# Layer 0's first projection in three parts with a border for each group of columns, x's squares first and on two engines, and five modulation chunks fetched without waiting for a buffer

## The chip, the cores and the metric

One core of a Trainium2 chip runs the whole program; the core has five engines with a queue of instructions each. TensorE (PE in the profile) multiplies matrices into PSUM, VectorE (DVE), ScalarE (ACT) and GpSimd (POOL) work element by element, and SyncE (SP) issues all DMAs here. The metric is the time of one execution on the device in microseconds (us).

## The reference

Two layers on x (256 tokens by 2048 channels, float32). What matters here is the first step of layer 0: a modulation vector from c, then the normalised and modulated h, then one wide projection of h.

```python
mod = c_act @ ada_w[l] + ada_b[l]                       # 6 x 2048 values
sh_a, sc_a, gt_a, sh_m, sc_m, gt_m = jnp.split(mod, 6)
h = rmsnorm(x, norm_mix[l]) * (1.0 + sc_a) + sh_a
qa, ka, va, qb, kb, vb, ga, gb = split_cols(h @ w_in[l])
...                                                     # two attentions, projections
merged = jax.nn.sigmoid(ga) * ya + jax.nn.sigmoid(gb) * yb
x = x + gt_a * (merged @ w_out[l])
h = rmsnorm(x, norm_ffn[l]) * (1.0 + sc_m) + sh_m
...                                                     # gated MLP with a convolution of width 3
```

## The kernel before

Channels lie on the 128 partitions: x and h are 16 chunks (kc 0 to 15) of 128 channels by 256 tokens. Products in float32 quality are made of three products: each operand is split into a high part and a rest, and high x high, high x rest and rest x high are added up.

**Weights** come as a stream of units: one unit is 16 blocks of 128x128, 1 MB, one DMA (L255). ACT copies each half of a unit to its high part (`hl`, L264) and DVE subtracts that from the weights for the rest (`hl`, L265). There are 4 such halves in buffers, so two units at most are split ahead of PE. A unit costs PE 24 matmuls of 512 columns (`tokens`, L331 to L333, for q, k and v: tokens on the partitions of the result) or 48 of 256 columns (`features`, L273 to L275, for the gates and the rest).

**Modulation** is not on PE: for each of 96 chunks of 128 values DVE multiplies a 1 MB chunk of `ada_w` (`aw`, 128x2048) by silu(c) and adds along the row (L196). Chunks come in the order shift 0, scale 0, shift 1, scale 1 and so on, so that h of chunk kc needs `aw` number 2kc and 2kc+1. The rows of `aw` and the units of weights share one pool of four 1 MB buffers (`raw`): a DMA into it is issued when DVE has read the buffer's last content.

**The start.** ACT squares x in four pieces (L611), DVE adds them up and folds them (L613, L615), PE sums over the partitions (L618), DVE adds epsilon (L619), POOL takes the power -0.5 (L394), PE spreads it over the partitions (L385) and ACT copies it out (`rbs`, L389). Then each chunk of h is one step of `normed`: DVE makes `ht` (L403), ACT adds the shift and rounds to the high part of h (L406), DVE makes the rest (L407).

**Layer 0's first projection.** The columns are nine groups of 512 (k and v of the first attention, then q, and so on) and 16 blocks of gate A. Since h comes chunk by chunk, the sum over kc is cut into four parts, of 2, 4, 5 and 5 chunks. In each part all nine groups and all 16 gate blocks get the products of these chunks. The first part's results are copied to SBUF by ACT (L751, L787), the later ones are added there by DVE (L753, L782). The last part then goes on to the norms of q and k, their transposes, the attention heads (in the background) and the sigmoid of the gates. So part 0 is 4.5 + 2 = 6.5 units, and all parts together are 52. Ahead of each part the code brings h up to the part's last chunk; in between, a background job makes 0.65 of a chunk of `aw` per unit. A scheduler puts each engine's instructions into a fixed order when the program is built; at run time each engine goes through its list and waits wherever an operand isn't there.

## Time and profile before

| | us |
|---|---|
| median of 3 runs (lowest, highest) | 2703.92 (2703.27, 2705.94) |
| the profiled execution | 2704.2 |
| its span | 2702.4 |
| PE busy in the span | 2660.9 (98%) |
| DVE busy | 2099.4 (78%) |
| ACT busy | 1411.0 (52%) |

PE is busy nearly throughout, so what can be lost or won lies where it isn't, or where its matmuls start further apart than elsewhere. In the view by stretches each row has a stretch in us, then for each engine its busy us and, in brackets, its instructions; then the clock that TensorE was granted, the share of the DMA engines' time and GB/s. In the view in order of time a row has start, length, engine, line, operation, result<-operands and, in square brackets, how long the engine had sat idle before and what ended that. The chain of waits names start, length and what stood on the path.

### The profile page before, as it was taken

To read this page: it belongs to the slowest core of one execution; us is meant where nothing else is said; L and a number is where in the kernel's file an instruction comes from. 1 tells how busy PE (TensorE), PEld (TensorE's weight loads), DVE (VectorE), ACT (ScalarE), POOL (GpSimd) and SP (SyncE) were. 2 spreads that over 40 slices of the span, in tenths; PEclk is the share of its full clock that TensorE was granted. 3 is DMA by queue.
4 is the path that set the end of the run, shared out by engine and by line. 5 is a ranking of instruction groups with operands and counts; after the bars stand their busy time and mean duration, and the time that the engine had idled before them with its cause. 6 is when DMAs were issued, how large, how long until landed. Compare 5 with 4: busy or idle time off the path is not lost.

```text
span 2702.4 us, 50217 instructions
## 1 busy us (share of the span) xinstructions
PE 2660.9 (98%) x21088; PEld 2565.8 (95%) x21088; DVE 2099.4 (78%) x2941; ACT 1411.0 (52%) x2081; POOL 35.1 (1%) x24
## 2 busy tenths in 40 slices
PE   7899999999999999999999999999999999999999
PEld 5688799999999999999998889999999999999999
DVE  6998987897987888788886666658879866655664
ACT  5344684455754455345564556544565445543553
POOL 0000100000000000000000000000000000000000
PEclk9899999999999999999999999999999999999999
DMA  8887578987688888878766656666757775555554
GB/s 319 329 340 272 218 288 313 356 309 265 235 296 297 291 293 286 296 290 297 291 217 250 241 209 231 233 237 254 292 184 283 285 265 197 188 200 190 190 200 142
DMA packets 101892, 700.38 MB, mean 259 GB/s; under 512 B 12705, under 2 KB 15009, under 8 KB 17697
## 3 DMA queue, kind: packets, MB, share of 16 engines
q1 hardware_dynamic: 101666, 697.17, 70.7%
q8 instruction: 165, 2.70, 0.4%
q14 instruction: 61, 0.50, 0.0%
HBM read 695.03 MB, written 2.10 MB: 258 GB/s over the span
## 4 chain that ended last, share of the span: by engine, by line
PE 91%; DVE 4%; DMA 1%; ACT 1%; POOL 1%; issue 1%; SPq 0%; POOLq 0%; ACTq 0%; DVEq 0%
PE ps L273 26%; PE ps L275 25%; PE ps L274 25%; PE ps_t L332 4%; PE ps_t L333 4%; PE ps_t L331 4%; DVE aw L196 1%; DVE hl L265 1%; PE po L559 1%; PE sc L528 1%; DMA aw<-in_aw 1%; POOL qrs L378 1%; PE tp L553 0%; ACT hl L264 0%; DVE qn L492 0%
## 5 line engine op out<-in xcount | busy, mean ns | idle before, releaser
L265 DVE TENSOR_TENSOR hl<-w,hl 128x1024 fp32r<-128x1024 f32 x928 | 1130.2, 1222 | 362.5 <-ACT hl L264 360.9
L264 ACT CAST hl<-w 128x1024 fp32r<-128x1024 f32 x928 | 971.1, 1049 | 771.9 <-PE ps L275 487.1
L273 PE MATMUL ps<-h,hl 128*128 128x256 f32 x3328 | 925.1, 278 | 0.0
L275 PE MATMUL ps<-h,hl 128*128 128x256 f32 x3328 | 923.6, 278 | 0.9 <-DVE hl L265 0.9
L274 PE MATMUL ps<-h,hl 128*128 128x256 f32 x3328 | 921.9, 277 | 0.0
L275 PEld LDWEIGHTS ps<-h,hl 128*128 128x128 f32 x3328 | 625.4, 188 | 1.5 <-DVE hl L265 1.3
L273 PEld LDWEIGHTS ps<-h,hl 128*128 128x128 f32 x3328 | 625.9, 188 | 0.5
L274 PEld LDWEIGHTS ps<-h,hl 128*128 128x128 f32 x3328 | 625.3, 188 | 0.4
L196 DVE CUSTOM_DVE_ANT_0 aw<-aw,cact,ab 128x2048 f32<-128x2048 f32 x192 | 450.8, 2348 | 62.8 <-DMA aw<-in_aw 62.0
L331 PE MATMUL ps_t<-hl,h 128*128 128x512 f32 x576 | 227.4, 399 | 7.9 <-ACT hl L264 7.3
L332 PE MATMUL ps_t<-hl,h 128*128 128x512 f32 x576 | 228.4, 397 | 5.2 <-DVE hl L265 5.2
L333 PE MATMUL ps_t<-hl,h 128*128 128x512 f32 x576 | 228.1, 396 | 0.9 <-DVE h L407 0.9
L858 DVE SCALAR_TENSOR_TENSOR u<-ps,cw,u 128x255 f32<-128x255 f32 x304 | 146.2, 481 | 68.0 <-ACT u L856 64.0
L856 ACT ACTIVATE u<-ps,cw 128x256 f32<-128x256 f32 x152 | 85.7, 564 | 185.6 <-PE ps L275 185.4
L275 PE MATMUL ps<-merged,hl 128*128 128x256 f32 x512 | 142.1, 278 | 0.0
L274 PE MATMUL ps<-merged,hl 128*128 128x256 f32 x512 | 141.8, 277 | 0.0
L273 PE MATMUL ps<-merged,hl 128*128 128x256 f32 x512 | 141.8, 278 | 0.0
L274 PE MATMUL ps<-act_o,hl 128*128 128x256 f32 x512 | 141.6, 277 | 0.0
L275 PE MATMUL ps<-act_o,hl 128*128 128x256 f32 x512 | 141.6, 276 | 0.0
L273 PE MATMUL ps<-act_o,hl 128*128 128x256 f32 x512 | 141.4, 277 | 0.0
L331 PEld LDWEIGHTS ps_t<-hl,h 128*128 128x128 f32 x576 | 109.5, 190 | 31.9 <-ACT hl L264 8.4
L332 PEld LDWEIGHTS ps_t<-hl,h 128*128 128x128 f32 x576 | 109.8, 191 | 30.9 <-DVE hl L265 8.2
(209 smaller groups left out, 4574.1 us busy)
## 6 DMA issues: line engine op xcount, KB each, us to landing
w<-in_ws SPq DMA_DIRECT2D x464, 1024.0 KB, 4.9
aw<-in_aw SPq DMA_DIRECT2D x192, 1024.0 KB, 5.7
bias<-in_bias SPq DMA_DIRECT2D x16, 256.0 KB, 4.5
x<-in_xT SPq DMA_DIRECT2D x4, 512.0 KB, 5.4
out<-x SPq DMA_DIRECT2D x16, 128.0 KB, 2.3
cw<-in_cw SPq DMA_DIRECT2D x2, 176.0 KB, 4.5
maskA<-in_maskA SPq DMA_DIRECT2D x1, 256.0 KB, 5.3
ab<-in_ab SPq DMA_DIRECT2D x2, 48.0 KB, 6.1
```

The source lines that it names most:

```text
L196: nc.vector.tensor_tensor_reduce(out=raw[:], in0=raw[:], in1=cact[:], scale=1.0, scalar=ab[:, i : i + 1], op0=ALU.mult, op1=ALU.add, accum ...
L264: nc.scalar.copy(hl[:, 0], r)
L265: nc.vector.tensor_tensor(out=hl[:, 1], in0=r, in1=hl[:, 0].bitcast(F32), op=ALU.subtract)
L273: nc.tensor.matmul(out, hi, act[0], start=first, stop=False)
L274: nc.tensor.matmul(ps[:, :S], hi, act[1], start=False, stop=False)
L275: nc.tensor.matmul(out, lo, act[0], start=False, stop=last)
L331: nc.tensor.matmul(ps[:], xh, hi, start=kc == kcs[0], stop=False)
L332: nc.tensor.matmul(ps[:], xh, lo, start=False, stop=False)
L333: nc.tensor.matmul(ps[:], xl, hi, start=False, stop=kc == kcs[-1])
L378: nc.gpsimd.tensor_tensor(out=dst, in0=src, in1=mhalf[:, :k], op=ALU.pow)
L856: nc.scalar.activation(out=u, in_=ps, func=AF.Identity, scale=w[:, 1:2], bias=w[:, 3:4])
L858: nc.vector.scalar_tensor_tensor(out=u[:, to], in0=ps[:, of], scalar=w[:, j : j + 1], in1=u[:, to], op0=ALU.mult, op1=ALU.add)
```

## The change

- **Parts and borders.** Layer 0 has three parts, and each group of columns has its own border between them: the first part takes kc 0 to 1 for the first three groups, 0 to 2 for two, 0 to 3 for four and 0 to 5 for the gates; the second goes on to 8, 8, 9, 10, 10, 11, 10, 10, 12 and 13. The first part is now 28/4 + 6 = 13 units, the second 15 + 7 = 22, the third 14 + 3 = 17, 52 as before. Every group waits for the chunks of h that it needs itself (`have_h`).
- **Rates.** The background job makes 1.1, 0.85 and 0.7 chunks per unit in the three parts.
- **Start.** x's squares carry high priority; pieces 0 and 2 are squared by ACT, 1 and 3 by DVE; epsilon is added by ACT; 8 and 12 idle matmuls (`warm`) stand before and after the sum over the partitions.
- **Buffers.** `aw` chunks 2, 3 and 4 of layer 0 are read into room that the outputs (`o`, `b1`) need only later, and the first unit of weights is fetched after `aw` 1.
- The small tables (mask, rotation, gains) are loaded in the second part.

```diff
-K_PARTS_0 = [2, 4, 5, 5]
-K_PARTS = [[range(sum(K_PARTS_0[:i]), sum(K_PARTS_0[: i + 1])) for i in range(len(K_PARTS_0))], [range(KC)]]
+K_ENDS = [
+    [([2, 2, 2, 3, 3, 4, 4, 4, 4], 6), ([8, 8, 9, 10, 10, 11, 10, 10, 12], 13), ([KC] * 9, KC)],
+    [([KC] * 9, KC)],
+]
+def k_parts(l):
+    parts, at, gat = [], [0] * len(QKV_GROUPS), 0
+    for ends, gend in K_ENDS[l]:
+        parts.append(([range(a, e) for a, e in zip(at, ends)], range(gat, gend)))
+        at, gat = ends, gend
+    return parts
...
-FIRST_RATE = 0.65
+FIRST_RATE = [1.1, 0.85, 0.7]
...
-WARM_IN = 6
+WARM_IN = [8, 12, 6]
+OWN = {2: "o", 3: "o", 4: "b1"}
...
         for n, i in enumerate(ADA_ORDER):
-            raw = rawp.tile([P, D], F32, name=f"aw{l}_{n}", tag="raw")
+            if l == 0 and n in OWN:
+                if OWN[n] not in own:
+                    own[OWN[n]] = [place(OWN[n], 16 if OWN[n] == "o" else 12, F32, f"aw_{OWN[n]}"), 0]
+                t, k = own[OWN[n]]
+                own[OWN[n]][1] += 1
+                raw = t[:, KC // 2 * k : KC // 2 * (k + 1)].rearrange("p k s -> p (k s)")
+            else:
+                raw = rawp.tile([P, D], F32, name=f"aw{l}_{n}", tag="raw")
...
-        nc.scalar.activation(out=sq[:], in_=x[:, i : i + 4], func=AF.Square)
+            if i // 4 % 2:
+                nc.vector.tensor_tensor(out=sq[:], in0=x[:, i : i + 4], in1=x[:, i : i + 4], op=ALU.mult)
+            else:
+                nc.scalar.activation(out=sq[:], in_=x[:, i : i + 4], func=AF.Square)
...
-    nc.vector.tensor_scalar(out=mean_sq[:], in0=ps[:], scalar1=EPS, scalar2=None, op0=ALU.add)
+        nc.scalar.activation(out=mean_sq[:], in_=ps[:], func=AF.Identity, bias=eps[:])
...
-            while done[0] < 2 * len(K_PARTS[0][0]):
+            while done[0] < 2:
+                next(job0)
+            st.prefetch(1)
+            while done[0] < 2 * K_ENDS[0][0][0][0]:
                 next(job0)
...
+        def have_h(part):
+            while l == 0 and done[0] < 2 * part.stop:
+                next(job0)
+        for pi, (groups, gates) in enumerate(parts):
             last = pi == len(parts) - 1
-            for g in range(len(QKV_GROUPS)):
+            if l == 0:
+                bg.pace(job0, FIRST_RATE[pi])
+            for g, part in enumerate(groups):
+                have_h(part)
                 pss = st.tokens(h, part)
-                if pi == 0 and g == 0:
+                if pi == max(0, len(parts) - 2) and g == 0:
                     gains, sink, cw, rots = small(l)
```

In the order lists below a name has its numbers: `aw0_5` is chunk 5 of layer 0, `w0_2` unit 2 of its weights, `hl0_2_1` the second half of unit 2, `ps0_7_t0` a result for the first 128 tokens; the last number only tells buffers apart.

SP's queue, from the first chunk of `aw` on. Before:

```order
L195 DMA aw0_0_150<-in_aw 128x2048
L195 DMA aw0_1_153<-in_aw 128x2048
L195 DMA aw0_2_175<-in_aw 128x2048
L195 DMA aw0_3_178<-in_aw 128x2048
L255 DMA w0_0_192<-in_ws 128x2048
L145 DMA maskA_212<-in_maskA 128x512
```

Now:

```order
L219 DMA aw0_0_174<-in_aw 128x2048
L219 DMA aw0_1_177<-in_aw 128x2048
L279 DMA w0_0_199<-in_ws 128x2048
L219 DMA aw_o_207<-in_aw 128x2048 x2
L219 DMA aw_b1_251<-in_aw 128x2048
L279 DMA w0_1_258<-in_ws 128x2048
L219 DMA aw0_5_280<-in_aw 128x2048
```

The first unit of weights moved from fifth to third place, and seven transfers stand ahead of the first one that needs a buffer back; before, it was four.

DVE's list from the second chunk of `aw` to the first splits of weights (`ISA` with `aw` is L196's multiply and sum; the short rows that read its sum out are left out). Before:

```order
L196 ISA aw0_1_153,mod0_144<-aw0_1_153,cact_94,ab0_145 128x2048
...
L619 TENSOR_SCALAR ms_in_125<-ss_in_139 128x2
...
L196 ISA aw0_2_175,mod0_144<-aw0_2_175,cact_94,ab0_145 128x2048
...
L403 SCALAR_TENSOR_TENSOR ht_171<-x_110,amod0_149,rbs_169 128x256
L196 ISA aw0_3_178,mod0_144<-aw0_3_178,cact_94,ab0_145 128x2048
...
L407 SCALAR_TENSOR_TENSOR h0_0_143<-ht_171,mod0_144,h0_0_143 128x256
...
L265 TENSOR_TENSOR hl0_0_0_194<-w0_0_192,hl0_0_0_194 128x1024
L407 SCALAR_TENSOR_TENSOR h0_0_143<-ht_182,mod0_144,h0_0_143 128x256
L265 TENSOR_TENSOR hl0_0_1_197<-w0_0_192,hl0_0_1_197 128x1024
```

Now:

```order
L220 ISA aw0_1_177,mod0_168<-aw0_1_177,cact_96,ab0_169 128x2048
...
L427 SCALAR_TENSOR_TENSOR ht_195<-x_112,amod0_173,rbs_193 128x256
L431 SCALAR_TENSOR_TENSOR h0_0_167<-ht_195,mod0_168,h0_0_167 128x256
L289 TENSOR_TENSOR hl0_0_0_201<-w0_0_199,hl0_0_0_201 128x1024
L289 TENSOR_TENSOR hl0_0_1_204<-w0_0_199,hl0_0_1_204 128x1024
L220 ISA aw_o_207,mod0_168<-aw_o_207,cact_96,ab0_169 128x2048
...
L427 SCALAR_TENSOR_TENSOR ht_213<-x_112,amod0_173,rbs_193 128x256
L220 ISA aw_b1_251,mod0_168<-aw_b1_251,cact_96,ab0_169 128x2048
...
L431 SCALAR_TENSOR_TENSOR h0_0_167<-ht_213,mod0_168,h0_0_167 128x256
```

The first chunk of h and both splits of unit 0 moved ahead of `aw` 2 and 3; the second chunk of h now ends behind three chunks of `aw` (2, 3 and 4).

DVE's list where h of chunk 7 is made. Before, this is at the border of parts 0 and 1, where h of chunk 5 is made ahead of unit 7:

```order
L196 ISA aw0_10_574,mod0_144<-aw0_10_574,cact_94,ab0_145 128x2048
...
L407 SCALAR_TENSOR_TENSOR h0_0_143<-ht_570,mod0_144,h0_0_143 128x256
L196 ISA aw0_11_577,mod0_144<-aw0_11_577,cact_94,ab0_145 128x2048
...
L403 SCALAR_TENSOR_TENSOR ht_581<-x_110,amod0_149,rbs_169 128x256
L196 ISA aw0_12_599,mod0_144<-aw0_12_599,cact_94,ab0_145 128x2048
...
L407 SCALAR_TENSOR_TENSOR h0_0_143<-ht_581,mod0_144,h0_0_143 128x256
L265 TENSOR_TENSOR hl0_7_0_604<-w0_7_602,hl0_7_0_604 128x1024
```

Now, inside part 0:

```order
L289 TENSOR_TENSOR hl0_9_1_656<-w0_9_651,hl0_9_1_656 128x1024
L220 ISA aw0_14_711,mod0_168<-aw0_14_711,cact_96,ab0_169 128x2048
...
L220 ISA aw0_15_714,mod0_168<-aw0_15_714,cact_96,ab0_169 128x2048
...
L427 SCALAR_TENSOR_TENSOR ht_718<-x_112,amod0_173,rbs_193 128x256
L431 SCALAR_TENSOR_TENSOR h0_0_167<-ht_718,mod0_168,h0_0_167 128x256
L289 TENSOR_TENSOR hl0_10_0_726<-w0_10_724,hl0_10_0_726 128x1024
```

Before, six chunks of `aw` stood between the splits of units 6 and 7 (numbers 7 to 12); now two at most stand between two splits after the first units.

More of the change, by code (lines that the diff above doesn't have):

```diff
@@ L79, in block_stream @@
             seq += [("w_in", kc, GATE_A // P + mo) for kc in range(KC)]
-    for part in K_PARTS[l]:
-        for g in QKV_GROUPS:
+    for parts, gates in k_parts(l):
+        for g, part in zip(QKV_GROUPS, parts):
             for kc in part:
@@ L84, in block_stream @@
         for mo in range(bare, KC):
-            seq += [("w_in", kc, GATE_A // P + mo) for kc in part]
+            seq += [("w_in", kc, GATE_A // P + mo) for kc in gates]
     for mo in range(KC):
@@ L156, in encoder @@
     x = const.tile([P, KC, S], F32, name="x")
-    skip(96, const)
+    skip(64, const)
     skip(224)
@@ L184, in encoder @@
     mods, amods, nrms, done = {}, {}, {}, {0: 0, 1: 0}
+    own = {}
     def ada(l):
@@ L600, in ada_and_h @@
             yield
-    for _ in range(FIRST):
-        next(adas)
     for i in range(0, KC, 4):
@@ L607, in encoder @@
     mean_sq = sm.tile([P, 2], F32, name="ms_in", tag="nsa")
[L608 to L619 removed]
+    with tc.high_priority():
+        acc = place("y0", 4, F32, "sq_in")
+        for i in range(0, KC, 4):
+            sq = acc if i == 0 else place(f"y{1 + i // 4 % 2}", 4, F32, f"sq_in{i}")
+            if i // 4 % 2:
+                nc.vector.tensor_tensor(out=sq[:], in0=x[:, i : i + 4], in1=x[:, i : i + 4], op=ALU.mult)
+            else:
+                nc.scalar.activation(out=sq[:], in_=x[:, i : i + 4], func=AF.Square)
+            if i:
+                nc.vector.tensor_tensor(out=acc[:], in0=acc[:], in1=sq[:], op=ALU.add)
+        for n in (2, 1):
+            nc.vector.tensor_tensor(out=acc[:, :n], in0=acc[:, :n], in1=acc[:, n : 2 * n], op=ALU.add)
+        warm(WARM_IN[0])
+        ps = ax.tile([P, 2], F32, name="ss_in", tag="ss", bufs=1)
+        for t in range(2):
+            tc.keep_in_program_order(
+                nc.tensor.matmul(ps[:, t : t + 1], acc[:, 0, t * P : (t + 1) * P], mean[:], start=True, stop=True)
+            )
+        warm(WARM_IN[1])
+        nc.scalar.activation(out=mean_sq[:], in_=ps[:], func=AF.Identity, bias=eps[:])
     tables = []
@@ L774, in encoder @@
                     bg.add(job, ATT[l])
+            have_h(gates)
             for mo in range(BARE[0] if l else 0, KC):
@@ L787, in gate_a @@
                         nc.scalar.copy(ya[:, mo], ps)
-                st.features([hs[k] for k in part], [gate_a])
+                st.features([hs[k] for k in gates], [gate_a])
         attended(HA)
```

23 lines of the change are left out of this document (5 added, 18 removed).

## The prediction

> **What bounds the kernel now.** I read the page's head first.
>
> ```profile
> span 2702.4 us, 50217 instructions
> PE 2660.9 (98%) x21088; PEld 2565.8 (95%) x21088; DVE 2099.4 (78%) x2941; ACT 1411.0 (52%) x2081; POOL 35.1 (1%) x24
> ```
>
> PE bounds the span, and both kernels give it the same products. So the change can move only the time in which PE gets nothing, or runs at half pace. That I look for by stretches of the start (PE's busy us comes second; the granted clock is the number after POOL).
>
> ```profile
> 26.40:67.20 40.80, 38.62 (x205) 32.74 (x206) 31.27 (x42) 27.82 (x48) 0.00 (x0) 0.96 0.80 297
> 67.20:81.40 14.20, 4.62 (x15) 2.35 (x14) 14.09 (x20) 3.78 (x6) 0.00 (x0) 0.73 1.01 387
> 81.40:87.40 6.00, 5.95 (x14) 4.70 (x15) 5.34 (x8) 1.99 (x2) 0.00 (x0) 0.50 0.95 384
> 87.40:147.00 59.60, 59.60 (x332) 52.23 (x332) 57.63 (x73) 24.42 (x26) 0.00 (x0) 1.00 0.84 307
> 147.00:160.00 13.00, 12.11 (x78) 10.70 (x78) 12.71 (x18) 4.39 (x5) 0.00 (x0) 1.00 0.90 348
> 255.00:450.00 195.00, 187.30 (x1252) 169.17 (x1251) 170.02 (x320) 133.53 (x244) 15.15 (x7) 0.99 0.70 260
> ```
>
> PE has nothing before 26.4, hardly anything from 67.2 to 81.4, where DVE (14.09 of 14.20) and the DMA engines (1.01) are full, and runs at half clock until 87.4. From 87.4 on it is full, with 0.9 us missing to 160 and 7.7 from 255 to 450 (the attention's part). To count the loss I need PE's pace:
>
> ```profile
> 45.22 0.40 PE L331 MATMUL ps_t<-hl,h 128*128 128x512 f32 x1
> ...
> 52.17 0.39 PE L331 MATMUL ps_t<-hl,h 128*128 128x512 f32 x1
> ...
> 79.12 1.22 PE L331 MATMUL ps_t<-hl,h 128*128 128x512 f32 x2 [6.99 <-ACT hl L264]
> ...
> 86.73 0.63 PE L333 MATMUL ps_t<-hl,h 128*128 128x512 f32 x1
> ```
>
> Between the first two rows lie 30 matmuls: 6.95/30 = 0.232 us each, so a unit (24 of them) takes 5.6 us. Until 67.1 part 0 was done, 6.5 units or 36.4 us of work; to 87.4 came 29 more matmuls (15 and 14 in the rows of stretches), 6.8 us. So 87.4 - 43.2 = 44.2 us were lost by then, and 44.2 + 0.9 + 7.7 = 52.8 us by 450.
>
> The chain of waits shows the first 29 us of it:
>
> ```profile
> 15.17 2.34 DVE aw L196
> ...
> 17.86 1.14 DVE aw L196
> ...
> 20.28 2.88 POOL nrs L394
> ...
> 23.21 0.70 PE rb L385 x2
> ...
> 23.93 0.38 ACT rbs L389
> ...
> 24.34 0.48 DVE ht L403
> 24.82 2.26 DVE aw L196
> ...
> 27.09 0.40 DVE h L407
> ...
> 28.00 1.23 DVE hl L265
> ...
> 29.27 0.68 PE ps_t L332
> ```
>
> Three chunks of `aw` stand on the path in DVE's list, between squares, sum and h. The gap at 67 to 81 is the border of part 1: six chunks of `aw` and their steps of h stand between two splits.
>
> **The change, step by step.** For the sums I need starts and paces of the other engines.
>
> ```profile
> 5.27 1.06 ACT L611 ACTIVATE sq_in<-x 128x1024 f32<-128x1024 f32 x1 [3.25 <-DMA x<-in_xT]
> ...
> 8.61 1.06 ACT L611 ACTIVATE sq_in<-x 128x1024 f32<-128x1024 f32 x1
> ```
>
> ```profile
> 9.70 1.23 DVE L613 TENSOR_TENSOR sq_in<-sq_in,sq_in 128x1024 f32<-128x1024 f32 x1 [8.56 <-ACT sq_in L611]
> ...
> 14.56 0.69 DVE L615 TENSOR_TENSOR sq_in<-sq_in 128x512 f32<-128x512 f32 x1
> ...
> 99.68 1.22 DVE L265 TENSOR_TENSOR hl<-w,hl 128x1024 fp32r<-128x1024 f32 x1
> 100.82 2.34 DVE L196 CUSTOM_DVE_ANT_0 aw<-aw,cact,ab 128x2048 f32<-128x2048 f32 x1
> 103.09 0.08 DVE L196 DVE_READ_ACCUMULATOR2_ANT mod<- 128x1 f32 x1
> 103.09 1.28 DVE L753 TENSOR_TENSOR packB<-ps_t,packB 128x512 f32<-128x512 f32 x2
> 104.29 0.15 DVE L203 SCALAR_TENSOR_TENSOR amod<-mod,nrm 128x1 f32<-128x1 f32 x1
> ```
>
> ```profile
> 42.29 2.00 ACT L264 CAST hl<-w 128x1024 fp32r<-128x1024 f32 x2
> ```
>
> ```profile
> 17.91 1.01 PE L618 MATMUL ss_in<-mean,sq_in 128*128 128x1 f32 x4 [7.55 <-DVE sq_in L615]
> ```
>
> ```profile
> 4.35 2.51 SPq L195 DMA_DIRECT2D aw<-in_aw  x4
> 17.55 0.33 SPq L255 DMA_DIRECT2D w<-in_ws  x1
> ```
>
> From one start to the next: a split 1.14 us, a chunk of `aw` 2.27, a pair of adds 1.20; a cast on ACT about 1.0; I take 0.4 for each of DVE's two operations of a step of h and for ACT's one between them (the chain's row of h).
>
> *Mean square.* Pieces of x land from 5.27 on, about 1.4 apart (0.52 MB at 387 GB/s). DVE squares piece 1 from 6.6 (my estimate) to 7.8 and adds to 9.0; ACT's second square (8.61 + 1.06) lets it add from 9.7 to 10.9; square 3 to 12.0, add to 13.2, folds to 14.2. Before, the last fold ended at 17.86, and epsilon waited to 20.05 behind `aw` 1. Now: 1.0 (PE) to 15.2, ACT's epsilon about 0.3, POOL 2.88 to 18.5, then 0.70 and 0.38: `rbs` at 19.6 instead of 24.3. Moving epsilon to ACT thus costs nothing: ACT has nothing else to do there. The 14 more `warm` matmuls lie in PE's two waits, for DVE and for POOL; at half pace the 12 (0.43 each) would end at 20.4 and cost up to 1.9, at full pace nothing. I take nothing.
>
> *First products.* h of chunk 0 is there at 21.0, the first split at 22.8, the second at 23.9 (before, the first matmul with a rest came at 29.27). The weights are no limit: `w0_0` was issued at 17.55 because it needed a buffer back, and now it goes third after x, 3 MB at 2.7 us each (1.05 MB at 387 GB/s). But h of chunk 1 stands behind `aw` 2, 3 and 4: 23.9 + 3 x 2.27 + 1.0 = 31.7. Until then PE can do 17 of its first 24 matmuls; it idles from 24.9 to 29.4 and falls back to half clock, as it had after the idle time ahead of 79.12. There matmuls were still 0.43 apart at 86.73, and full soon after. I take half clock from 29.4 to 34.9: 31.7 - 17 x 0.232 = 27.7 lost, and 1.5 more: **29.2**, where before stood 26.4 + 4.4 at the end of part 0, and then the gap.
>
> A rule speaks against this order of steps. The Trainium skill, "TensorE: Matmul & The Clock Gate", section "What's actually happening", says that the clock falls to half after an idle window of about 3.4 us and is full again after about 3.4 us of work, which would make the earlier `warm` matmuls useless here too. By that figure the half clock would end at 32.8, and the sum would be 1.0 lower. The trace agrees on the fall and needs longer for the return, 8 us from 79.12.
>
> *The gap at 67 to 81* (14.2 + half clock) goes: the first three groups need two chunks of h, the gates six, and DVE makes them while PE has work. What is late next is single splits. I followed the new lists of DVE and ACT, each instruction at the end of the one ahead of it or of its operand, with the paces above:
> - unit 2's first half stands behind `aw` 6 and the step of chunk 2: 37.6 + 2.3 + 1.9 = 41.8, PE is done with unit 1 at 40.3: 1.5;
> - unit 3's second half behind `aw` 8: 1.0;
> - unit 10 behind `aw` 14, `aw` 15 and the step of chunk 7: 2 x 2.27 + 1.3 + 1.14 = 7.0 us between splits, with 4.0 us of PE work in hand: 3.0;
> - five smaller ones: 1.1. Together **6.6** in part 0.
> - Part 1: `aw` 20 between the adds of group 0 and unit 15's split: 1.20 + 2.27 + 1.14 less the 3.3 of PE work left and the 0.4 by which the first add comes earlier: 0.9; the splits right behind group 7 and group 8, where no half is left in hand: 0.7 and 1.9. **3.5**.
> Such stalls are unsure: between 87.4 and 147, with DVE at 57.63 of 59.60, PE didn't wait once.
>
> One round of copies and adds falls away (nine pairs and 16 gates). DVE isn't the limit by its sum: to the end of unit 27 it does 32 x 2.27 + 56 x 1.14 + 16 x 0.9 + 9 x 1.20 = 162 us from 14.2, to 177 and some 5 for its early waits, when PE is at 28 x 5.6 + 39.3 = 196.
>
> *Part 2* has 17 units instead of 16.25, with 6.2 chunks per group on average instead of 5, so more PE work lies between two groups' norms, whose work on DVE is the same. Of the 7.7 lost there I take 2 off: **5.7**; bounds are 0 and, with the rival below, 12.
>
> Sum: 29.2 + 6.6 + 3.5 + 5.7 = 45.0 against 52.8: 7.8 us less. From the profiled execution's own 2704.2 (0.3 above the median 2703.9) this gives **2696**. The second layer's list is the same in kind; I give it nothing.
>
> **Rivals.**
> 1. *The small stalls don't come*, since ACT and DVE run ahead as between 87.4 and 147. Then 10 us of them stay away: 2686 to 2690. Against it: `aw` 14 and 15 back to back leave no way round.
> 2. *The late part gives it back.* The gates' last turn is now 3 units instead of 5, with 16 sigmoids and the heads' exponentials on ACT, which was full there already:
>
> ```profile
> 345.00:360.00 15.00, 13.78 (x108) 13.01 (x107) 14.88 (x32) 14.40 (x27) 0.00 (x0) 1.00 0.75 280
> 360.00:375.00 15.00, 14.75 (x118) 14.09 (x117) 12.27 (x27) 14.88 (x29) 0.00 (x0) 1.00 0.79 307
> ```
>
>    At 98% of ACT's time (14.40 + 14.88 of 30), the same 16 gates' work in 11 us less can cost up to 6: 2702, no change that can be told.
> 3. *Slower, by ACT's list.* Each step of h waits on DVE for ACT, whose list has copies ahead of it that wait for PE's next result; DVE then splits nothing. My walk finds 0.4 to 0.6 for it, twice. There are 14 steps after the second; if each cost PE 1 us or more beyond the sum, 14 us would be lost: 2710. It decides from 0.6 us per step. Against it: from 26.4 to 67.2, with such copies on the same list, PE missed 2.2 us in all (38.62 of 40.80).
> 4. *Nothing changes at the start*, if squares and h don't get ahead: the lists exclude it for the squares; the buffers alone would change little.
>
> **How the numbers follow.** Two runs differ by about 0.2% (5.4 us) at most where nothing changed. Forecast (2692 to 2699) 0.54; rival 1 0.18; rival 2 and other losses up to no change 0.20; rival 3 0.08. Faster: 0.54 + 0.18 = 0.72. Range: rival 1's better half and rival 3 left out, 2688 to 2703.
>
> **What would show it.** In the changed kernel: `rbs` at 19 to 20; PE idle 24 to 29 and again until 31.7; a full PE from 35 with stalls of 1 to 3 us at units 2, 3 and 10; no gap near 67; PE lost 36 us at the end of part 0 and 39 at the end of part 1. If PE is full through part 0, rival 1 holds; if ACT is full and PE waits in the last gates, near the end of the first projection, rival 2. A sum that fails altogether would show as PE waiting for `hl` with DVE idle behind ACT.

## The result and the profile after

The changed kernel took 2703.16 us (median of 14 runs, 2700.72 to 2708.59), the kernel before, run beside it, 2705.40 (14 runs, 2700.64 to 2709.96). The ratio is 0.9996, with a 95% interval of 0.9988 to 1.0004: 1 us less, somewhere between 3 less and 1 more. The forecast was 7.8 less. In the profiled execution (2700.7 us) little is left of the gain either:

```profile
span 2698.9 us, 50255 instructions
PE 2665.7 (99%) x21128; PEld 2565.9 (95%) x21128; DVE 2089.7 (77%) x2909; ACT 1405.0 (52%) x2078; POOL 32.6 (1%) x24
```

The span is 3.5 us shorter than before (2702.4). PE's 4.8 us more go with 40 more instructions, all of them `warm` matmuls in the start's idle time, so busy time can't be compared directly.

The view by stretches of the kernel after, cut at what was forecast (same columns as before):

```profile
24.60:29.60 5.00, 0.39 (x3) 0.03 (x1) 4.93 (x7) 0.59 (x2) 0.00 (x0) 0.79 1.01 421
29.60:34.40 4.80, 4.80 (x11) 3.62 (x12) 4.80 (x5) 2.51 (x4) 0.00 (x0) 0.50 0.80 329
34.40:110.70 76.30, 70.39 (x435) 61.97 (x434) 65.45 (x73) 40.78 (x63) 0.00 (x0) 0.98 0.88 338
67.20:81.40 14.20, 13.37 (x95) 12.40 (x94) 12.04 (x15) 6.83 (x11) 0.00 (x0) 1.00 0.87 350
110.70:238.90 128.20, 123.44 (x699) 104.92 (x698) 110.07 (x145) 49.35 (x54) 0.00 (x0) 1.00 0.84 311
```

The gap is gone: between 67.2 and 81.4 PE is busy for 13.37 us instead of 4.62. In its place PE now idles from 24.6 to 29.6, runs at half clock (0.50) until 34.4, and lacks 5.9 us to 110.7 and 4.8 us to 238.9, spread over thirteen small stalls (the view of waits below has 4 + 3 + 4 + 2 of them).

The same in order of time, the rows that mark the stages (`rbs`; the first matmul; the first one with h of chunk 1; the first of part 1, of part 2 and of the projection behind the attention):

```profile
18.22 0.37 ACT L413 COPY rbs<-rb 128x256 f32<-128x256 f32 x1 [2.74 <-PE rb L409]
...
21.37 0.73 PE L355 MATMUL ps_t<-hl,h 128*128 128x512 f32 x2 [1.85 <-ACT hl L288]
...
29.57 0.80 PE L355 MATMUL ps_t<-hl,h 128*128 128x512 f32 x1 [4.61 <-ACT h L430]
...
110.68 0.40 PE L355 MATMUL ps_t<-hl,h 128*128 128x512 f32 x1
...
238.86 0.40 PE L355 MATMUL ps_t<-hl,h 128*128 128x512 f32 x1
...
363.80 0.28 PE L297 MATMUL ps<-oA,hl 128*128 128x256 f32 x1
```

In the kernel before, the first matmul behind 35 units (36 matmuls of 256 columns ahead of its last part) and the last of these rows stood here:

```profile
239.34 0.28 PE L273 MATMUL ps<-h,hl 128*128 128x256 f32 x1
...
368.75 0.28 PE L273 MATMUL ps<-oA,hl 128*128 128x256 f32 x1
```

At the pace of 0.232 us, 13 units are 72.4 us and 35 are 194.9. So 38.3 us were lost at the end of part 0 (110.7 - 72.4) and 44.0 at the end of part 1 (238.9 - 194.9). Before, at 35 units, it was 44.5 by the row above (239.34 - 194.9); the prediction's working, with a rounded pace, has 45.1. The whole reshaping of parts and start won 0.5 us over these 35 units. Of the 4.95 us by which the projection begins earlier, some 3 are no gain at all: part of a head's work is now done behind that point, and that stage takes 65.6 us instead of 62.7. At its end 2.0 us are left.

Who made PE wait, and who made the DMA queue wait (the view of waits of the kernel after, PE from 30 to 240, SP from 30 to 112; columns: us in all, how often, the longest):

```profile
PE ps_t L355 <- ACT h L430: 4.6, 1, 4.6
PE ps_t L356 <- DVE hl L289: 3.3, 4, 1.5
PE ps L297 <- ACT hl L288: 3.1, 3, 2.6
PE ps_t L355 <- ACT hl L288: 2.5, 4, 1.5
PE ps L299 <- DVE hl L289: 1.3, 2, 0.8
```

```profile
SPq L279 <- DVE hl L289: 19.5, 6, 4.2
SPq L279 <- DVE mod L220: 17.5, 4, 6.1
SPq L219 <- DVE mod L220: 14.9, 3, 11.0
SPq L219 <- DVE amod L227: 10.4, 5, 2.1
SPq L219 <- DVE hl L289: 8.7, 5, 4.5
SPq L279 <- DVE amod L227: 4.3, 2, 2.2
```

The 4.6 us row is the wait for h of chunk 1 at 29.57. All others are waits for the next split half of the weights. And the queue that loads the weights and the `aw` chunks stands waiting for DVE to hand back a `raw` buffer for 75.3 of 82 us; in the kernel before it is 74.7 of the same 82, so this figure alone tells nothing of the change. The first view names ACT and DVE as those PE waits for; what these two were waiting for is the question of the experiments.

### The profile page after: what moved, and what is told of

Read it like the earlier page. It is cut to its first block, busy times and chain, and to the rows that moved or that the text cites. A ratio compares the mean times of both kernels' runs of the same rounds, so it can differ in the third digit from the quotient of the medians.

```text
span 2698.9 us, 50255 instructions
## 1 busy us (share of the span) xinstructions
PE 2665.7 (99%) x21128; PEld 2565.9 (95%) x21128; DVE 2089.7 (77%) x2909; ACT 1405.0 (52%) x2078; POOL 32.6 (1%) x24
## 4 chain that ended last, share of the span: by engine, by line
PE 86%; DVE 8%; ACT 2%; DMA 2%; issue 2%; POOL 1%; SPq 0%; DVEq 0%; ACTq 0%; POOLq 0%
PE ps L297 25%; PE ps L299 25%; PE ps L298 25%; PE ps_t L356 3%; PE ps_t L357 3%; PE ps_t L355 3%; DVE hl L289 3%; DVE aw L220 2%; DMA aw<-in_aw 1%; ACT hl L288 1%; PE po L583 1%; PE sc L552 1%; POOL qrs L402 1%; PE tp L577 0%; DVE qn L516 0%
## 5 line engine op out<-in xcount | busy, mean ns | idle before, releaser
L220 DVE CUSTOM_DVE_ANT_0 aw<-aw,cact,ab 128x2048 f32<-128x2048 f32 x189 | 443.6, 2348 | 55.1 <-DMA aw<-in_aw 54.4
```

Source lines behind the costliest of these rows:

```text
L220: nc.vector.tensor_tensor_reduce(out=raw[:], in0=raw[:], in1=cact[:], scale=1.0, scalar=ab[:, i : i + 1], op0=ALU.mult, op1=ALU.add, accum ...
```

## The experiments

The expectations name their theories by letters. D: VectorE's work sets the pace of parts 0 and 1. A: ScalarE's fixed list does, where casts stand behind copies that wait for PE, or behind the rounding of h, which waits for VectorE. M: the loads of `aw` and of the weights do, through the four `raw` buffers. A letter that isn't in this list is explained where it stands. In the table all times come first; "part 0", "part 1" and "projection" are the starts of the rows that end part 0 and part 1 and begin the projection behind the attention, in each run's own profile. The ratio is to the kernel before, run on the same chip.

| run | median us (lowest, highest) | ratio, 95% | part 0 | part 1 | projection |
|---|---|---|---|---|---|
| changed kernel | 2703.16 (2700.72, 2708.59) | 0.9996 (0.9988, 1.0004) | 110.7 | 238.9 | 363.8 |
| start_only | 2702.46 (2698.70, 2705.18) | 0.9994 (0.9985, 1.0004) | 66.8 | 152.1 | 367.9 |
| parts_only | 2704.09 (2700.95, 2706.24) | 0.9996 (0.9986, 1.0006) | 111.4 | 239.3 | 364.1 |
| h_on_dve | 2704.76 (2702.48, 2710.34) | 1.0005 (0.9994, 1.0015) | 116.0 | 244.4 | 369.2 |
| aw_half | 2700.09 (2695.28, 2702.73) | 0.9982 (0.9973, 0.9992) | 113.6 | 237.9 | 362.7 |
| aw_dma_half | 2690.46 (2687.99, 2692.09) | 0.9943 (0.9928, 0.9958) | 103.8 | 227.2 | 352.2 |
| aw_both_half | 2683.58 (2681.54, 2687.52) | 0.9920 (0.9904, 0.9935) | 97.9 | 221.0 | 346.0 |
| split_first | 2701.86 (2699.92, 2704.87) | 0.9988 (0.9979, 0.9997) | 110.0 | 238.2 | 363.0 |
| rate_09 | 2697.04 (2693.60, 2703.30) | 0.9971 (0.9961, 0.9981) | 107.8 | 235.4 | 360.4 |
| parts_09 | 2696.73 (2694.66, 2697.59) | 0.9971 (0.9961, 0.9982) | 107.6 | 235.1 | 359.9 |
| no_own | 2700.14 (2699.07, 2703.84) | 0.9987 (0.9978, 0.9996) | 111.7 | 239.6 | 364.7 |
| raw3 | 2728.20 (2725.75, 2732.84) | 1.0090 (1.0077, 1.0104) | 121.5 | 254.1 | 376.6 |
| rate_low | 2691.41 (2690.22, 2692.36) | 0.9952 (0.9939, 0.9964) | 106.7 | 231.1 | 355.0 |
| rates_only | 2692.79 (2690.79, 2694.25) | 0.9959 (0.9946, 0.9973) | 107.6 | 232.1 | 356.4 |
| before_dma_half | 2696.90 (2693.82, 2699.44) | 0.9973 (0.9964, 0.9982) | 67.1 | 145.6 | 359.3 |

(start_only and before_dma_half have the four parts of before, so their part ends aren't comparable with the others'; the kernel before has 67.1, 152.9 and 368.7.)

### Which half of the change

The new start (squares, matmuls for the clock, own buffers, first unit early) with the old parts:

```diff
-    [([2, 2, 2, 3, 3, 4, 4, 4, 4], 6), ([8, 8, 9, 10, 10, 11, 10, 10, 12], 13), ([KC] * 9, KC)],
+    [([e] * 9, e) for e in (2, 6, 11, KC)],
...
-FIRST_RATE = [1.1, 0.85, 0.7]
+FIRST_RATE = [0.65] * 4
...
-                if pi == max(0, len(parts) - 2) and g == 0:
+                if pi == 0 and g == 0:
```

> The changed kernel with the old four parts (2, 4, 5, 5 chunks, one border for all groups) and the old rate 0.65: only the start (squares first and on two engines, epsilon on ACT, idle matmuls, own buffers, first unit fetched early) is left of the change. Theory D (in parts 0 and 1 DVE, with its waits for ACT, sets the pace, and PE is fed at that pace): the gap at the first border stays, since it ends when DVE has made 12 chunks of aw; DVE's first chunk starts at 14.4 instead of 15.2 and some early waits go, so the gap ends 1 to 4 us earlier than 81.4 and the time is 1 to 4 us below the kernel before. Rival L (the start's gain is carried on whole, and what was lost later comes from single splits): 5 to 6 us below.

And the new parts with the old start:

```diff
-WARM_IN = [8, 12, 6]
-OWN = {2: "o", 3: "o", 4: "b1"}
+WARM_IN = [0, 0, 6]
+OWN = {}
...
-            while done[0] < 2:
-                next(job0)
-            st.prefetch(1)
```

and x's squares as in the kernel before.

> The changed kernel with the start as before the change (squares by ACT alone and in the old order, epsilon on DVE, no more idle matmuls, no own buffers, first unit not fetched early): only the parts with their borders, the rates and the later small tables are left. Theory D: no gap near 67, but part 0 ends only 0 to 3 us later than the changed kernel's 110.7, since DVE has the same list of work; time within 3 us of the changed kernel. Rival L: the start's 5 us are missing in full, part 0 ends at 115 to 117 and the time is 4 to 6 us above the changed kernel.

Neither half moves the time: 0.9994 and 0.9996. The start alone has its first matmul at 22.5 instead of 26.4 and gives it all back by the end of part 0 (66.8 against 67.1). The parts alone reach the projection 4.6 us earlier than before, and the new start adds 0.3 to that. Its first matmuls show why:

```profile
26.18 1.22 PE L355 MATMUL ps_t<-hl,h 128*128 128x512 f32 x2
29.09 0.50 PE L356 MATMUL ps_t<-hl,h 128*128 128x512 f32 x1 [1.70 <-DVE hl L289]
```

With the old start PE begins at 26.2 and, after a wait of 1.7 us, has both chunks of h. With the new start it begins at 21.4, has used up chunk 0 by 25.0 and waits until 29.57 for chunk 1. Both are back at work at about 29.

### Is it the sums, or ScalarE's part in h?

DVE instead of ACT rounds h's high part in layer 0's first projection, so that DVE has no wait for ACT within a step of h:

```diff
-            nc.scalar.activation(out=h[kc][:, 0], in_=t[:], func=AF.Identity, bias=sh)
+            if l == 0 and w == 0:
+                nc.vector.tensor_scalar(out=h[kc][:, 0], in0=t[:], scalar1=sh, scalar2=None, op0=ALU.add)
+            else:
+                nc.scalar.activation(out=h[kc][:, 0], in_=t[:], func=AF.Identity, bias=sh)
```

> The changed kernel, but DVE itself rounds h to its high part in layer 0's first norm (0.4 us more of DVE per chunk), so that a step of h waits for ACT no longer. In the changed kernel each step costs DVE some 0.6 us of waiting for ACT's h and 0.45 for the cast queued behind it. Theory D: DVE gains 0.4 to 0.7 us per step; part 0 ends 3 to 5 us earlier (106 to 108 instead of 110.7), part 1 5 to 8 us earlier (231 to 234 instead of 238.9), and the time falls by 4 to 8 us. Rival L: only the three stalls at a step of h shrink, by 2 us together; time within 2 us. A third theory, that half clock and late first chunks are what is left: nothing changes after 35 us.

Parts 0 and 1 end 5 us later. The scheduler also put DVE's list into another order around these steps, so this run says only that the waits of h on ACT weren't a price that could simply be taken off.

Then VectorE's own work was cut: the first 32 `aw` chunks of layer 0 are summed over half their columns (the other half is left out), 1.28 us instead of 2.34 each, the loads left whole:

```diff
-                out=raw[:], in0=raw[:], in1=cact[:], scale=1.0, scalar=ab[:, i : i + 1],
+                out=raw[:, : D // 2] if l == 0 and n < 32 else raw[:], in0=raw[:, : D // 2] if l == 0 and n < 32 else raw[:],
+                in1=cact[:, : D // 2] if l == 0 and n < 32 else cact[:], scale=1.0, scalar=ab[:, i : i + 1],
```

> The changed kernel with work left out: the first 32 modulation chunks of layer 0 multiply and sum only 1024 of their 2048 columns (about 1.2 instead of 2.34 us each on DVE; the DMAs are the same), so shift and scale are wrong. DVE has 36 us less to do in parts 0 and 1. Theory D: PE is full from the first chunks on; h of chunk 1 comes 3.4 us earlier; part 0 ends at 98 to 103 instead of 110.7, part 1 at 223 to 228 instead of 238.9, and the time falls by 9 to 14 us. Rival L: as D in part 0, since the same stalls shrink (it can't be told apart there). If ACT's list or the DMA engines set the pace (22 MB/us aside, 94% of the DMA time is used in stretches of part 0), part 0 ends above 106.

```profile
30.00:112.00 82.00, 74.37 (x429) 62.46 (x428) 53.97 (x75) 41.46 (x64) 0.00 (x0) 0.96 0.87 329
```

From 30 to 112 us DVE is busy for 54.0 us instead of 71.2, and PE gets no more done: 74.37 us busy, in the changed kernel 75.94 (its row stands below). Part 0 ends 2.9 us later, the projection begins 1.1 earlier. Theory D, as far as it means the sum of VectorE's work, is refuted: with 17 us taken off VectorE, PE waits as much, 10.8 us from 34.4 to 240 where the changed kernel has 10.2. They aren't the same waits, though (18 instead of 13).

### Loads against sums

Only the loads are halved: columns 0 to 1023 are loaded, and the sum over them is taken twice, which keeps DVE's time:

```diff
-            nc.sync.dma_start(raw[:], a["aw"][l, n])
-            nc.vector.tensor_tensor_reduce(
-                out=raw[:], in0=raw[:], in1=cact[:], scale=1.0, scalar=ab[:, i : i + 1],
-                op0=ALU.mult, op1=ALU.add, accum_out=mod[:, i : i + 1],
-            )
+            less = l == 0 and n < 32
+            w = D // 2 if less else D
+            nc.sync.dma_start(raw[:, :w], a["aw"][l, n][:, :w])
+            for _ in range(2 if less else 1):
+                nc.vector.tensor_tensor_reduce(
+                    out=raw[:, D - w :], in0=raw[:, :w], in1=cact[:, :w], scale=1.0, scalar=ab[:, i : i + 1],
+                    op0=ALU.mult, op1=ALU.add, accum_out=mod[:, i : i + 1],
+                )
```

> Work left out: of the first 32 aw chunks of layer 0 only columns 0 to 1023 are loaded (512 KB instead of 1024 KB), and the sum over these is taken twice into the same word, so that VectorE's time stays about as it was (2 x 1.28 instead of 2.34 us). So only the transfers become less, by half a MB a chunk, some 1.3 us at the 395 GB/s that 364 GB/s at a share of 0.92 means: 15 to 18 us by the end of part 0. Theory M (the transfers are the limit: share 0.84 to 0.93 in parts 0 and 1, and a w buffer is free late and lands late): the small stalls of the changed kernel go, part 0 ends at 104 to 107 instead of 110.7, part 1 at 231 to 235 instead of 238.9, time 2696 to 2699. Theory A (ScalarE's fixed list: casts stand behind copies that wait for TensorE, and behind the rounding of h that waits for ht): nothing moves, part 0 ends at 110 to 113, time 2701 to 2705. Theory D (VectorE's sum), already weakened: 0.22 us more a chunk, part 0 ends 2 to 4 later.

And both halved (the same load, one sum over `[:, :w]`):

> Work left out: of the first 32 aw chunks of layer 0 only columns 0 to 1023 are loaded and summed (512 KB and 1.28 us instead of 1024 KB and 2.34 us). Beside the run that halves the sums alone (part 0 ended at 113.6, part 1 at 237.8, median 2700.1) and the one that halves the loads alone it makes a square of four. Theory M: at least as early as with the loads alone halved, part 0 at 102 to 106. If VectorE and the transfers are each a limit as soon as the other is taken away, only this run is early (part 0 at 102 to 106, time 2694 to 2697) and the two single ones are not. Theory A: no earlier than with the sums alone halved, part 0 at 111 to 114, time 2699 to 2702.

The stretch 30 to 112 of the changed kernel, of the run with halved loads, and of the run with both:

```profile
30.00:112.00 82.00, 75.94 (x448) 65.84 (x448) 71.15 (x78) 43.55 (x67) 0.00 (x0) 0.95 0.88 338
```

```profile
30.00:112.00 82.00, 80.12 (x479) 70.78 (x480) 77.10 (x125) 44.43 (x69) 0.00 (x0) 0.96 0.79 267
```

```profile
30.00:112.00 82.00, 81.91 (x502) 72.55 (x501) 65.58 (x100) 47.93 (x73) 0.00 (x0) 1.00 0.86 305
```

With half the bytes, and with DVE even busier (77.1), PE is busy for 80.1 of 82 us; what is missing is nearly all the wait for chunk 1 of h. Its waits from 30 to 240, and DVE's longest row in the same stretch, first of the changed kernel:

```profile
DVE hl L289 <- ACT hl L288: 15.3, 22, 1.4
```

and of the run with halved loads:

```profile
PE ps_t L358 <- ACT h L433: 5.0, 1, 5.0
PE ps_t L359 <- DVE hl L292: 0.6, 1, 0.6
PE ps L302 <- DVE hl L292: 0.2, 1, 0.2
...
DVE hl L292 <- ACT hl L291: 16.4, 19, 1.5
```

PE's waits for split weights fall from 10.2 us to 0.8, although DVE waits as long as before for ACT's casts (16.4 against 15.3). At the projection, halved sums give 1.1 us, halved loads 11.6, both 17.8. So with half the bytes the stalls go. That the loads had held PE up isn't shown by it, because the lists changed with the loads. This is what waited for loads from 30 to 112, DVE's sums and ACT's casts in the changed kernel, then the casts with halved loads:

```profile
DVE aw L220 <- DMA aw<-in_aw: 0.6, 1, 0.6
```

```profile
ACT hl L288 <- DMA w<-in_ws: 0.5, 2, 0.3
```

```profile
ACT hl L291 <- DMA w<-in_ws: 23.1, 10, 4.3
```

In the changed kernel the two engines waited for loads for 1.1 us there, while PE waited 5.7 us for splits. With halved loads the casts wait far longer for loads, and PE for no split. The longest of the small stalls, 2.61 us ahead of unit 10's first matmul at 92.15, shows what held it. DVE and ACT of the changed kernel:

```profile
85.28 2.35 DVE L220 CUSTOM_DVE_ANT_0 aw<-aw,cact,ab 128x2048 f32<-128x2048 f32 x1
...
87.55 2.35 DVE L220 CUSTOM_DVE_ANT_0 aw<-aw,cact,ab 128x2048 f32<-128x2048 f32 x1
...
90.14 0.48 DVE L427 SCALAR_TENSOR_TENSOR ht<-x,amod,rbs 128x256 f32<-128x256 f32 x1
```

```profile
90.66 0.51 ACT L430 ACTIVATE h<-ht,mod 128x256 fp32r<-128x256 f32 x1 [0.70 <-DVE ht L427]
91.07 1.98 ACT L288 CAST hl<-w 128x1024 fp32r<-128x1024 f32 x2
```

Unit 10's load was issued at 80.50 and landed 7.5 us later, at 88.0, before PE ran dry at 89.5. Its cast stands on ACT's list behind a rounding of h, and that waits for two sums back to back on DVE's list: the place that the prediction named. With halved loads the same cast stands behind a copy and starts when its load lands:

```profile
82.63 1.05 ACT L291 CAST hl<-w 128x1024 fp32r<-128x1024 f32 x1 [3.29 <-DMA w<-in_ws]
```

So three things changed at once in that run: half the bytes, another order of the lists, and sums in two pieces, between which DVE's list can put a split. The run with halved sums alone has short pieces too and gained next to nothing, which speaks against the pieces. Bytes and order aren't separated by any run here.

The casts and subtractions of the first 36 units were then put ahead of everything not yet placed, the work unchanged:

```diff
-            nc.scalar.copy(hl[:, 0], r)
-            nc.vector.tensor_tensor(out=hl[:, 1], in0=r, in1=hl[:, 0].bitcast(F32), op=ALU.subtract)
+            with urgent(l == 0 and u < 36):
+                nc.scalar.copy(hl[:, 0], r)
+                nc.vector.tensor_tensor(out=hl[:, 1], in0=r, in1=hl[:, 0].bitcast(F32), op=ALU.subtract)
```

> The changed kernel with the same work; only the order: in layer 0's first 36 units the cast and the subtraction of a w half are put ahead of everything that is not yet placed, so on ScalarE both casts of a unit stand ahead of the copies of the products of the unit before (unit 1's second cast ahead of four copies of packA, unit 3's ahead of three of packB), and on VectorE both subtractions ahead of the next sum. Theory A: a split no longer waits for TensorE's group, the stalls at the ends of groups go, part 0 ends at 105 to 107 instead of 110.7, time 2697 to 2700. Theory M, and the theory that the four halves of split weights are the limit: a cast that stands earlier waits for a free half or for its transfer instead, part 0 ends at 110 to 112, time 2702 to 2705.

Part 0 ends 0.7 us earlier, not 4 to 6. Unit 1's second cast, which stood behind copies, now starts at 30.3 instead of 35.3, and little comes of it. But the edit didn't move a cast ahead of a rounding of h. At unit 10 the order is as it was, and PE waits 2.76 us there (2.61 in the changed kernel):

```profile
89.07 0.51 ACT L431 ACTIVATE h<-ht,mod 128x256 fp32r<-128x256 f32 x1 [0.86 <-DVE ht L428]
89.48 1.98 ACT L289 CAST hl<-w 128x1024 fp32r<-128x1024 f32 x2
```

Its load had been issued at 79.21 and had landed 6.4 us later. So this run doesn't test whether roundings of h ahead of casts set the pace.

### Fewer loads beside the early units, and fewer buffers

The rate of the modulation in part 0, 0.9 instead of 1.1, with the new start (rate_09) and with the old one (parts_09):

```diff
-FIRST_RATE = [1.1, 0.85, 0.7]
+FIRST_RATE = [0.9, 0.85, 0.7]
```

> The changed kernel with 0.9 instead of 1.1 steps of the modulation per unit in part 0, so some two or three aw chunks fewer beside its 13 units (each 2.34 us of VectorE and 2.6 us of transfer), which come later. Theory M or D: fewer small stalls in part 0, it ends 2 to 5 us earlier (106 to 109); what is left of that at the first projection depends on part 1, which gets the chunks: 362 to 364, time 2701 to 2704. Theory A: part 0 ends as before, 110 to 111, or earlier only by the h steps that moved out (0.5 us each).

> The start of the kernel before (x's squares on ScalarE alone, no own buffers, no matmuls for the clock) with the new parts, and the modulation's rate in part 0 at 0.9 instead of 1.1. Theory M (the loads of aw and w and the buffers that they land in set the pace of parts 0 and 1): the start is worth nothing there, so this run is as early as the run with the rate alone changed: part 0 ends at 107 to 109 (107.8 there), the first projection begins at 360 to 362 (360.4 there), time 2696 to 2700. If the new start carries its 5 us once the pace is looser, this run is 3 to 5 us later than that one: 364 to 366, time 2700 to 2702.

Two `aw` sums fewer beside 13 units (17 begun by the end of part 0 instead of 19) are worth 2.9 us at the end of part 0 and 6 us of the median (2697.04 against 2703.16). And the old start is as fast as the new one, 2696.73: the start is worth nothing at either rate, as theory M had it. That doesn't single out the loads, since a lower rate takes loads, sums and steps of h away together. The stretch 85 to 100, first of the changed kernel, then of rate_09:

```profile
85.00:100.00 15.00, 12.39 (x93) 12.00 (x91) 11.99 (x14) 6.14 (x10) 0.00 (x0) 0.89 0.95 362
```

```profile
85.00:100.00 15.00, 15.00 (x132) 15.00 (x131) 13.09 (x13) 8.28 (x14) 0.00 (x0) 1.00 0.96 369
```

`aw` 14 and 15 no longer stand back to back ahead of unit 10 (a sum starts at 90.12, the next at 96.08), and the wait there is gone, with as much loaded in the stretch (369 against 362 GB/s).

The own buffers alone taken away:

```diff
-OWN = {2: "o", 3: "o", 4: "b1"}
+OWN = {}
```

> The changed kernel with the first modulation chunks 2, 3 and 4 in the common ring of four buffers again, the rest of the new start kept. Theory M: three loads less run ahead of the ring in the first 20 us, so the transfers' share between 10 and 30 us falls from 1.01 to 0.85 to 0.98, and a w load or an aw load comes some 2.5 us later; the stalls up to 60 us grow by 1 to 3 us, part 0 ends at 111 to 113, time 2703 to 2705. If the own buffers do nothing, part 0 ends at 110.7 and the time stays at 2703.

The ends of the parts came as expected, some 1 us later, but the time didn't: 2700.14, where 2703 to 2705 was expected. So the own buffers win nothing that these runs can show.

Three `raw` buffers instead of four:

```diff
-    rawp = pool("raw", 4)
+    rawp = pool("raw", 3)
```

> The changed kernel with three buffers for w and aw instead of four (own buffers kept, no work changed). If the number of buffers and when VectorE frees them set the pace, the share of the transfers falls (0.85 to 0.70 or less between 30 and 112 us), part 0 ends at 118 to 130 and the time rises to 2712 or more. If it is the rate of the transfers alone (1024 KB in 2.5 us at the 423 GB/s of the first 30 us, two units of 2.5 us to 5.6 us of TensorE), three buffers keep two transfers under way and little is lost: part 0 at 111 to 114, time 2703 to 2708.

```profile
30.00:112.00 82.00, 68.87 (x366) 57.05 (x365) 62.86 (x77) 37.33 (x57) 0.00 (x0) 0.93 0.79 296
```

PE gets 68.87 instead of 75.94 us of work, part 0 ends 10.8 us later, part 1 15.2, and the whole kernel, whose weights all go through these buffers, takes 25 us longer. DVE is less busy (62.86) and so are the DMA engines (0.79): no engine is full, and everything is slower. Here the engines do wait for loads: DVE's sums 4.1 us from 30 to 112 instead of 0.6, ACT's casts 2.1 instead of 0.5, and PE's waits from 34.4 to 240 come to 19.9 us instead of 10.2. So three buffers are too few. That four are too few as well doesn't follow, and five weren't tried.

The best version, rates of 0.9 and 0.75 in parts 0 and 1 and the splits ahead, and the rates alone:

```diff
-FIRST_RATE = [1.1, 0.85, 0.7]
+FIRST_RATE = [0.9, 0.75, 0.7]
```

> The changed kernel with rates of 0.9 and 0.75 instead of 1.1 and 0.85 in parts 0 and 1, and the casts and subtractions of the first 36 units placed ahead (as in the run with only that). Theory M: the modulation's loads are spread evenly over part 1 instead of being over by its unit 18; its stalls (5.6 us in the changed kernel, about 6 with 0.9 alone) fall to 3 to 4 us, part 1 ends at 232 to 234, the first projection begins at 357 to 360, time 2693 to 2697. If part 1's demand for h (10 chunks for its fourth group, 13 for its gates) bites, a gap of 2 to 5 us stands ahead of the groups with 10 and 11 chunks, and the time is 2697 to 2700.

> The changed kernel with rates of 0.9 and 0.75 alone, nothing placed ahead. With both the first projection began at 355.0 and the time was 2691.4; with 0.9 alone 360.4 and 2697.0; with the casts and subtractions placed ahead alone 363.0 and 2701.9 (the changed kernel: 363.8 and 2703.2). Theory M: the rates carry it, 355.5 to 357, time 2692 to 2694. If the order carries the rest once the pace is looser, 359 to 361, 2696 to 2698.

The stretch 112 to 240, first of the changed kernel, then of the version with both edits:

```profile
112.00:240.00 128.00, 123.38 (x698) 105.16 (x697) 109.20 (x145) 49.63 (x53) 0.00 (x0) 1.00 0.83 310
```

```profile
112.00:240.00 128.00, 125.65 (x714) 109.88 (x713) 111.89 (x141) 50.75 (x54) 0.00 (x0) 1.00 0.85 320
```

PE misses 2.4 us there instead of 4.6. The two rates alone bring 2692.79, with the order of the splits 2691.41: 13 us less than the kernel before and 11.7 less than the changed one, by the medians. Of the 11.7 the rates carry 10.4. The same number of `aw` chunks is loaded by the end of part 1 in all these kernels; they only come more evenly.

### Was the kernel before held by the loads too?

The same halving of loads in the kernel before:

> Work left out: in the kernel before, too, only columns 0 to 1023 of the first 32 aw chunks are loaded, and their sum is taken twice (as in the run of the changed kernel with halved loads, which was at part 0's end 6.9 us and at the first projection 11.6 us earlier than with whole loads). Theory M for both kernels: before is held by the same loads, so it gains as much: the first projection begins at 355 to 359 instead of 368.75, time 2689 to 2694. If the gap of before at 67 to 81 us is VectorE's (six sums back to back, 14.09 of 14.20 us busy), it stays, and before gains only 2 to 5 us: 364 to 367, time 2700 to 2702. Then the loads became the limit only when the gap was taken away.

The result lies between the two expectations: the projection begins 9.5 us earlier, the time falls by 6.8. 7.3 us of the 9.5 are there by the end of its second part (145.6 instead of 152.9), and they come from the gap, where PE now works more:

```profile
67.20:81.40 14.20, 10.77 (x35) 7.63 (x34) 13.32 (x23) 5.40 (x8) 0.00 (x0) 0.76 0.80 292
```

against 4.62 us. But DVE's list changed with it: four and a half sums instead of six stand in the gap. So how much of the gap is the loads and how much the six sums stays open.

## Why the prediction was wrong

**Mean square and first products.** `rbs` was ready at 18.6 (19.6 forecast); that 1.0 is luck, since POOL took 1.79 us where the sum has 2.88. PE was idle from 25.0 to 29.6 (24.9 to 29.4), the rest of h of chunk 1 was made at 31.2 to 31.6, and full clock came at 34.4 (34.9). 12 matmuls started ahead of the idle time and 11 at half clock, so 34.4 - 23 x 0.232 = 29.1 us were lost by then (29.2 forecast). Mechanism, times and size came out. (The `warm` matmuls added are 20, not 14.) The forecast had itself left little for the start (29.2 against 30.8), and the runs show that it is nothing. On the clock, the Trainium skill, "TensorE: Matmul & The Clock Gate", section "What's actually happening", gives about 3.4 us of work until full clock is back; here it took 4.8 us after the idle time (29.57 to 34.40) and 3.7 us after the wait at unit 10 (92.15 to 95.82), so the Trainium skill's figure was the lower end of what was seen.

**The gap** went, as forecast.

**The failed step is the sizing of the small stalls: "6.6 in part 0" and "3.5" in part 1.** They measured 9.2 (38.3 - 29.1) and 5.7 (44.0 - 38.3), 4.8 us more together. The places that it named were right: PE waited 1.55 us at unit 2 (1.5 forecast), 0.77 at unit 3's second half (1.0), 2.61 at unit 10 (3.0), 1.47 at unit 15 behind `aw` 20 (0.9), 0.79 behind group 7 (0.7) and 0.99, in three pieces, behind group 8 (1.9). All thirteen waits from 34.4 to 240 are 10.2 us of idle time, and the forecast had 10.1; that single terms were off both ways and the sum came out so close is in part luck. What the walk left out is what comes with a wait. The wait at unit 10 brought the clock down:

```profile
89.54:92.15 2.61, 0.00 (x1) 0.00 (x0) 1.51 (x6) 1.86 (x4) 0.00 (x0) 1.00 1.02 358
92.15:95.80 3.65, 3.65 (x16) 3.46 (x17) 3.65 (x3) 0.90 (x1) 0.00 (x0) 0.53 0.86 337
```

At a granted clock of 0.53 the matmuls of 256 columns start 0.21 us apart instead of 0.116, which lost about 1.7 us in 3.65; the prediction had half clock in its sum for the start alone. In rate_09, where that wait is gone, the clock stays full there (1.00 from 85 to 100). And each wait costs more than its idle time, as the matmul ahead of it runs out: 89.27 to 92.15 is 2.76 us above the pace for 2.61 of idle time, 39.95 to 41.89 is 1.71 for 1.55. At 0.16 for each of 13 waits that is an estimate of 2.1 us. So 10.2 + 1.7 + 2.1 = 14.0 of the 14.9 are accounted for; the rest is open.

Another term that the walk left out is the way round of a `raw` buffer: DVE frees it, the load is issued, it lands 6 to 7 us later, and only then can ACT cast. The view of loads of the kernel after, from 30 to 112 (number of loads, size, median us from issue to landing):

```profile
aw<-in_aw SPq DMA_DIRECT2D x13, 1024.0 KB, 7.3
w<-in_ws SPq DMA_DIRECT2D x12, 1024.0 KB, 6.2
```

The walk took every load as landed when its cast was due. In part 0 that nearly held (0.5 and 0.6 us of waiting for loads). In part 1 it didn't: from 110.7 to 238.9 the casts waited 19.7 us for loads, in 8 waits, of which PE felt little, as it waited 4.4 us in all. That less loading helps is measured (halved loads, lower rates); that it helps through these buffers, and not through the order of the lists that came with it, stays open.

How near the transfers' own rate is as a limit can be told roughly: the queue moved 421 GB/s at a share of 1.01 while PE idled, and 338 GB/s at 0.88 in part 0. The Trainium skill, "DMA: Bandwidth & Descriptors", section "Where 436 GB/s comes from", gives 435 GB/s as the ceiling of the way into SBUF and about 358 as a core's share of the memory; this core, the only one that this program uses, went past the second and nearly up to the first. So part 0 ran at four fifths of what the transfers had shown they can do, and their rate was not the limit there.

**Part 2** was to win 2.0. It took 124.9 us for 17 units, before 125.1 for 16.25, which is 4.3 better by the pace; but 2.95 of it is head work that moved behind it, so 1.4 remains.

**The sum**: 0.5 in parts 0 and 1 and 1.4 in part 2 are 1.9 us (2.0 by the rows behind the next stage), and 3.5 at the trace's end, where 7.8 was forecast; the medians show 2.2, the ratio 1.1. Of the 5.9 us between 7.8 and 1.9, the small stalls are 4.8, the base at 35 units 0.6 (45.1 against 44.5) and part 2 0.6; the start's 0.1 goes the other way. The prediction also held that two runs of one kernel differ by 5.4 us at most; the 14 runs of the kernel before lie 9.3 us apart (2700.64 to 2709.96).

**The rivals.** Rival 1 (no small stalls) is what the kernel with halved loads does, though with other lists as well. Rival 2 put the loss into the late part; the loss lies in parts 0 and 1, so its time was near and its reason wrong. Rival 3 (ACT's list) had a real wait in view, casts and splits that a step of h holds up, but the forecast's own walk had priced the same places at about what they measured as idle time, and nothing near rival 3's 14 us came of them.

## What to carry to other kernels

A forecast that adds up small waits must price what comes with them: here 10.2 us of waiting lost 14.9, and 1.7 of that came from one wait of 2.6 us, after which the clock was at half. A large gap between two parts may only be the same late work gathered in one place, and spreading it won 0.5 us of 14 here. A queue that waits for buffers nearly all the time is no sign of a limit by itself: it did so for 74.7 of 82 us before, 75.3 after and 67.8 with halved loads, where PE hardly waited. Where leaving out work also gives the scheduler other lists, compare the lists before the gain is put down to the work. What helped was to ask for less beside the tight stretch: a lower rate of the background chunks won 10 us with one line, after a restructuring that won none.

## What was not expected

- Taking the three own buffers away made the ends of the parts 1 us later and the time 3 us shorter by the medians (2700.14 against 2703.16). The intervals of the two ratios overlap (0.9978 to 0.9996 and 0.9988 to 1.0004), so the second isn't shown.
- POOL's power of two columns took 2.87 us in the kernel before, 1.79 in the changed one and 1.38 in the run without own buffers, for the same instruction on the same shape.
- Moving one small operation per chunk of h from ACT to DVE cost 5 us by the end of part 0. The scheduler also chose another order, and which of the two cost it stays open.
